# A fused two-layer trunk with a 16-expert mixture: experts put in order of their token count on the chip, the small ones run as plain fp32 products in two column halves

## The chip, the cores and the metric

The kernel runs on one core of a Trainium2 chip. The metric is the device time of one execution in microseconds (us). Its engines are named in the profile as PE (matrix products), PEld (the loads of PE's stationary operand), DVE (elementwise work), ACT (activations and copies), POOL (here mostly indirect DMA) and SP (which issues nearly all of the other DMAs, in order).

## What the kernel computes

Two layers of a trunk: each has a mixer of three branches over 256 tokens of x and 256 of a context, and then a mixture of experts. Layer 0's mixture runs over 512 tokens (x and context), layer 1's over 256 (x alone). The change concerns the mixture:

```python
def hierarchical_moe(h, w_router_group, w_router_expert, w1, w3, w2):
    g_logits = (h @ w_router_group).astype(jnp.float32)
    g_sel = jnp.argmax(g_logits, axis=-1)                      # one of 4 groups
    ...
    top_vals, top_idx = lax.top_k(e_in_group, MOE_TOPK)        # 2 of its 4 experts
    top_w = jax.nn.softmax(top_vals, axis=-1) * g_gate
    ...
    for e in range(MOE_EXPERTS):                               # 16
        hid = jax.nn.silu(h @ w1[e]) * (h @ w3[e])             # 1024 -> 512
        out = out + (hid @ w2[e]) * gates[:, e:e + 1]          # 512 -> 1024
    return out
```

Everything is fp32, to fp32 accuracy. With these inputs the router gives the 16 experts of layer 0 101, 88, 84, 83, 82, 80, 76, 67, 65, 61, 56, 53, 39, 32, 29 and 28 tokens (in falling order), and those of layer 1 75, 69, 42, 39, 36, 31, 28 (four times), 22, 20, 19, 18, 17 and 12.

## The kernel before

Only the routed tokens of an expert are computed, in up to `CAP` = (128, 96) slots per expert in layers 0 and 1. Experts run in the order 0 to 15. For each one POOL gathers its token rows from DRAM (`gather`, L1466), PE transposes them (`tokens`, L1523), and the result is split into a high and a low part. All weights are fp32 and come in pieces of 1 MB (`wload`, L221): two for w1, two for w3, two for w2, so six per expert and 96 per layer. SP issues them in a fixed order (`pieces_of`, L1239), w1's first piece half an expert ahead. A piece is issued when a slot of the ring of buffers is free; some 13 slots in layer 0 and 14 in layer 1 are filled ahead of the routing, and four of them leave the ring after 50 pieces (`CUT`).

Each half piece is split on the chip into a high and a low part (`split`): ACT rounds it (L241, `whi`), DVE subtracts (L242, `wlo`). Every 128x512 tile of a weight then takes three products:

```python
    def mm3(self, out, lh, ll, rh, rl, start, stop):
        mm(out, lh, rh, start=start, stop=False)               # L211
        mm(out, lh, rl, start=False, stop=False)               # L212
        self.mm = mm(out, ll, rh, start=False, stop=stop)      # L213
```

That is 72 products for an expert: 24 for w1, 24 for w3 (`up`, L1528) and 24 for w2. Between them stand 8 transposes of the tokens, tanh on ACT (L1547), two multiplications on DVE (L1548, L1549) and 4 transposes of the hidden rows (L1552). The output rows, scaled by the gate (`ye`, L1586), are scattered to DRAM (`yb`, L1471). The last two experts' rows stay on chip (L1593, L1594); the other rows are read back (L1601), added in pairs on POOL (L1602), and PE puts both together (L1613, L1616), which is the head of a tail of some 15 us in the last layer.

Routing, before all this: one-hot choices on DVE, a prefix count by products on PE (L1394, L1397), the first expert's tokens selected by products with a one-hot (L1415), the slot lists of four experts (one-hots on DVE L1442, products on PE L1444), then token numbers `tki` (L1452) for the gathers. If any expert has more than `CAP` tokens, a branch (L1621) computes the rest in a general way; with these counts it is not taken.

The order on each engine comes from a scheduler that works from its own estimates; PE, DVE and SP run their queues strictly in it.

## Time and profile before

| what | value |
|---|---|
| time, median of 3 runs | 1622.67 us (1621.13 to 1624.53) |
| span of the profiled execution | 1619.3 us |
| PE busy in it | 94% |
| DVE busy | 74% |
| ACT busy | 60% |
| granted TensorE clock, mean | 0.982 of full |

The span runs from the first to the last instruction; the 3.4 us to the median lie around it. The profile has no total time of the profiled execution of its own beside the span, so sums below are made in the span and carried over to the median with those 3.4 us. A busy share is a mean over all stages: what a stage costs is read from its own stretch. The two mixtures run from about 640 to 948 us and from about 1303 to 1602 us.

### The profile page before, as it was taken

What the parts mean: (1) busy time and instruction counts of PE and PEld (TensorE: products, weight loads), DVE (VectorE), ACT (ScalarE), POOL (GpSimd) and SP (SyncE); (2) the same over time, 40 slices, a digit from 0 to 9 for tenths busy, and PEclk for the clock granted to TensorE, in tenths of its full rate; (3) what the DMA queues carried; (4) which work ended last, traced back from release to release, by engine and by line L of the source; (5) the groups of instructions that cost most, each with busy time, mean ns of one, the idle gap of its engine ahead of it and who ended that gap; (6) DMA issues with size and microseconds to landing.
All of it is one profiled execution on the core that took longest, in us unless ns stands there. A gap on an engine that the chain in (4) does not pass through costs nothing. (4 is left out here: it accounts for less than half of the span.)

```text
span 1619.3 us, 23310 instructions
## 1 busy us (share of the span) xinstructions
PE 1518.8 (94%) x8530; PEld 1163.3 (72%) x8530; DVE 1197.5 (74%) x1943; ACT 971.8 (60%) x1530; POOL 245.5 (15%) x244
## 2 busy tenths in 40 slices
PE   6999899999999996999999979998999799999996
PEld 4666665677777796778888748777799767767763
DVE  4479677432476766999999966478855689999996
ACT  4668465322223333888888835577744468888883
POOL 2034100000121103111111031032011121101011
PEclk9999999999999998999999989999999899999999
DMA  9762333443456586999799836223244979989991
GB/s 314 227 195 79 131 105 105 147 150 121 153 180 213 176 301 247 334 374 373 283 371 372 312 112 189 79 79 105 82 145 155 364 269 367 365 303 322 368 362 40
DMA packets 219215, 363.05 MB, mean 224 GB/s; under 512 B 26405, under 2 KB 101359, under 8 KB 219092
## 3 DMA queue, kind: packets, MB, share of 16 engines
q1 hardware_dynamic: 211232, 349.68, 62.7%
q0 software_dynamic: 7424, 11.67, 2.1%
q8 instruction: 71, 1.16, 0.3%
q14 instruction: 52, 0.43, 0.1%
q10 hardware_dynamic: 436, 0.10, 0.0%
HBM read 352.97 MB, written 23.40 MB: 232 GB/s over the span
## 5 line engine op out<-in xcount | busy, mean ns | idle before, releaser
L242 DVE TENSOR_TENSOR wlo<-wraw,whi 128x1024 fp32r<-128x1024 f32 (+1 forms) x514 | 615.3, 1216 | 153.7 <-ACT whi L241 89.1
L241 ACT ACTIVATE whi<-wraw 128x1024 fp32r<-128x1024 f32 (+1 forms) x514 | 523.4, 1029 | 271.0 <-PE pa L205 116.1
L204 PE MATMUL pa<-hhi,whi 128*128 128x512 f32 (+1 forms) x704 | 241.1, 357 | 1.6 <-ACT kT L768 0.8
L205 PE MATMUL pa<-hlo,whi 128*128 128x512 f32 (+1 forms) x704 | 238.4, 353 | 0.1
L212 PE MATMUL pa<-wlo,xh 128*128 128x512 f32 (+1 forms) x480 | 194.6, 405 | 3.0 <-DVE wlo L242 2.8
L211 PE MATMUL pa<-whi,xh 128*128 128x512 f32 (+1 forms) x480 | 191.0, 398 | 0.2 <-ACT xh L247 0.2
L213 PE MATMUL pa<-whi,xl 128*128 128x512 f32 (+1 forms) x480 | 189.6, 395 | 0.0
L204 PEld LDWEIGHTS pa<-hhi,whi 128*128 128x128 f32 x704 | 133.8, 190 | 36.2 <-issue 16.1
L207 PE MATMUL pa<-hhi,wlo 128*128 128x512 f32 (+1 forms) x704 | 151.2, 348 | 0.0
L205 PEld LDWEIGHTS pa<-hlo,whi 128*128 128x128 f32 x704 | 134.0, 190 | 23.1 <-issue 9.6
L207 PEld LDWEIGHTS pa<-hhi,wlo 128*128 128x128 f32 x704 | 113.4, 189 | 20.2 <-issue 6.2
L212 PEld LDWEIGHTS pa<-wlo,xh 128*128 128x128 f32 (+1 forms) x480 | 84.0, 175 | 31.8 <-DVE wlo L242 8.3
L212 PE MATMUL c<-wlo,hh 128*128 128x512 f32 (+1 forms) x256 | 101.5, 396 | 3.7 <-DVE wlo L242 3.7
L211 PEld LDWEIGHTS pa<-whi,xh 128*128 128x128 f32 (+1 forms) x480 | 83.9, 175 | 26.3 <-ACT xh L247 0.3
L739 POOL TENSOR_TENSOR m<-m,gu 128x512 f32<-128x512 f32 (+1 forms) x32 | 39.8, 1242 | 406.0 <-DVE gu L737 406.0
L213 PEld LDWEIGHTS pa<-whi,xl 128*128 128x128 f32 (+1 forms) x480 | 84.2, 175 | 21.6
L211 PE MATMUL c<-whi,hh 128*128 128x512 f32 (+1 forms) x256 | 97.7, 398 | 0.4 <-ACT hh L247 0.2
L1466 POOL DMA_INDIRECT xg<-h2b,tki x30 | 45.8, 1528 | 343.4 <-PE c L1523 285.9
L212 PE MATMUL pa<-y,whi 128*128 128x512 f32 (+1 forms) x192 | 66.8, 348 | 0.9 <-DVE y L248 0.9
L211 PE MATMUL pa<-y,whi 128*128 128x512 f32 (+1 forms) x192 | 66.1, 345 | 0.7 <-DVE mx L1119 0.7
L213 PE MATMUL pa<-y,wlo 128*128 128x512 f32 (+1 forms) x192 | 65.5, 342 | 0.0
L325 DVE SCALAR_TENSOR_TENSOR adaw<-adaw,cT 128x512 f32<-128x512 f32 x56 | 47.1, 842 | 17.4 <-DMA adaw<-in_w_ada_dram 16.8
(471 smaller groups left out, 2807.2 us busy)
## 6 DMA issues: line engine op xcount, KB each, us to landing
wraw<-in_w_dram SPq DMA_DIRECT2D x182, 1024.0 KB
wraw<-in_w_in_dram SPq DMA_DIRECT2D x44, 1024.0 KB
adaw<-in_w_ada_dram SPq DMA_DIRECT2D x80, 512.0 KB
x<-in_w_dram SPq DMA_DIRECT2D x10, 1024.0 KB
adaw<-in_w_ada_dram SPq DMA_DIRECT2D x8, 1024.0 KB
wraw<-in_w_out_dram SPq DMA_DIRECT2D x8, 1024.0 KB
yb<-zero SPq DMA_DIRECT2D x12, 512.0 KB
wraw<-yb SPq DMA_DIRECT2D x6, 1024.0 KB
```

The source lines that it names most:

```text
L204: mm(out, lh, rh, start=(i == 0), stop=False)
L205: mm(out, lh, rl, start=False, stop=False)
L207: self.mm = mm(out, ll, rh, start=False, stop=(i == len(ops) - 1))
L211: mm(out, lh, rh, start=start, stop=False)
L212: mm(out, lh, rl, start=False, stop=False)
L213: self.mm = mm(out, ll, rh, start=False, stop=stop)
L241: self.sp = nc.scalar.activation(hv[:, :, q], v[:, :, q], AF.Copy)
L242: self.sl = self.lo.tensor_sub(lv[:, :, q], v[:, :, q], hv[:, :, q].bitcast(F32))
L325: nc.vector.scalar_tensor_tensor(v[:, j], v[:, j], ck, acc, op0=OP.mult, op1=OP.add)
L739: nc.gpsimd.tensor_add(self.m[:, j, :], self.m[:, j, :], u[:, :TY])
L1466: return nc.gpsimd.indirect_dma_start(out=xgs[e % len(xgs)][:cap], out_offset=None, in_=h2b, in_offset=bass.IndirectOffsetOnAxis(ap=tki[:c ...
```

## The change

All experts keep their six 1 MB pieces. The 16 experts of a layer get *places*, given by a string: `B` for a place whose expert runs as before (128 slots, split weights, 72 products) and `s` for a small place. In layer 0 five of the places are small, in layer 1 eleven. The first two places of layer 0 (three of layer 1) always hold experts 0, 1 (and 2), so that their weights can be loaded ahead of the routing; the others are given out by token count, ranked on the chip, the largest to the `B` places. SP then reads the expert's number from memory into a register (L1272) and addresses the weight pieces with it. The fallback branch is taken if a place holds more than its slots (128 or 64); with these counts it is not.

An expert at a small place has 64 slots and no split: its weights go into the products as they are, as plain fp32. Its 64 tokens fill half of the array's columns; w1 is multiplied in columns 0 to 63 and w3 in columns 64 to 127, and the two column halves of w2's 1024 outputs likewise (`pair`, L1643). That makes 24 products in 12 pairs in place of 72, 8 transposes of 64 rows, a copy of w3's half (ACT), and 4 transposes of the hidden rows; the output rows are scattered as half rows. In the routing the prefix count for expert 0 alone comes first, then the ranking on DVE, and then a second prefix count over the places. The diff, cut to its core:

```diff
-CAP = (128, 96)
+CAP = (128, 128)
+SM = 64
+
+STAT = (2, 3)
+PLACES = ("BBsBBsBBsBBsBsBB", "BBBsssssssssssBB")
...
+    pos = np.zeros((P, 2, 5, NE), f)
+    for l in range(2):
+        big = np.array([x == "B" for x in PLACES[l]])
+        pos[:, l, 0] = NE - 1 - np.arange(NE) + 1.0e5 * np.maximum(0, STAT[l] - np.arange(NE))
+        pos[:, l, 1] = place_ranks(l)
+        pos[:, l, 2] = np.where(big, CAP[l], SM)
+        pos[:, l, 3] = np.where(big, 1, 2)
+        pos[:, l, 4] = (~big)[None, :] * (np.arange(P) >= SM)[:, None]
...
+    n = STAT[l] + PLACES[l][STAT[l]:].count("B")
+    big, small = iter(range(n)), iter(range(n, NE))
+    return [next(big if x == "B" else small) for x in PLACES[l]]
...
+        def src(w, q):
+            if q < STAT[l]:
+                return self.io[w][l, q]
+            if q not in self.eid:
+                self.eid[q] = self.nc.values_load(self.idi[0:1, q:q + 1], engines=(mybir.EngineType.SP,),
+                                                  min_val=0, max_val=NE - 1)
+            return self.io[w][l][bass.ds(self.eid[q], 1)].rearrange("e r c -> (e r) c")
...
+        def begin(q):
+            for w in ("w1", "w3")[:1 + (PLACES[l][q] == "s")]:
+                yield up(w, q, 0)
+        self.eid = {}
+        yield from begin(0)
+        for q in range(NE):
+            yield up("w1", q, 1)
+            if PLACES[l][q] == "B":
+                yield up("w3", q, 0)
+            yield up("w3", q, 1)
+            if q + 1 == STAT[l]:
+                yield from down(q)
+            if q + 1 < NE:
+                yield from begin(q + 1)
+            if q + 1 != STAT[l]:
+                yield from down(q)
...
-        pc = self.c2()
+        self.behind(self.rest, V.tensor_add(Mb, O[:, 0], O[:, 1]))
+
+        def prefix(pc, m, n):
+
+            for t in range(nt):
+                for u in range(t + 1):
+                    nc.tensor.matmul(pc[:, ts(t, n)], self.trilb if u == t else self.onesb, m[:, u, :n],
+                                     start=(u == 0), stop=(u == t))
+        p0 = self.c2()
+        prefix(p0, Mb, 1)
...
+            nc.tensor.matmul(p0[:, ts(1, NE)], self.onesb, Mb[:, u, :], start=(u == 0), stop=(u == nt - 1))
+
+        pm0 = tl([P, nt], "pm0")
+        V.scalar_tensor_tensor(pm0, p0[:, :nt], 1.0, Mb[:, :, 0], op0=OP.add, op1=OP.mult)
...
+        V.scalar_tensor_tensor(key, p0[:, ts(1, NE)], float(NE), pos[:, 0], op0=OP.mult, op1=OP.add)
+        cmp = self.xp.tile(kb, F32, name="cmp")
+        V.tensor_tensor(cmp, key[:, None, :].to_broadcast(kb), key[:, :, None].to_broadcast(kb), op=OP.is_gt)
+        V.reduce_sum(rank, cmp, axis=AX.X)
+        V.tensor_tensor(cmp, rank[:, None, :].to_broadcast(kb), pos[:, 1][:, :, None].to_broadcast(kb), op=OP.is_equal)
+        V.tensor_tensor(cmp, cmp, self.iotab[:, None, :NE].to_broadcast(kb), op=OP.mult)
+        idf = tl([P, NE], "idf")
+        V.reduce_sum(idf, cmp, axis=AX.X)
+        self.idi = tl([P, NE], "idi", I32)
+        V.tensor_scalar(self.idi, idf, -1.0, None, op0=OP.add)
...
+        V.tensor_tensor(Q, O, rank[:, None, None, :].to_broadcast(rb), op=OP.mult)
+        V.reduce_sum(rk, Q, axis=AX.X)
+        V.tensor_tensor(Q, rk[:, :, :, None].to_broadcast(rb), pos[:, 1][:, None, None, :].to_broadcast(rb), op=OP.is_equal)
+        V.tensor_add(Mb, Q[:, 0], Q[:, 1])
+        pc = self.c2()
+        prefix(pc, Mb, NE)
...
+        V.scalar_tensor_tensor(pm, pcv, 1.0, Mb, op0=OP.add, op1=OP.mult)
...
         def scatter(ye, e):
-            return nc.gpsimd.indirect_dma_start(out=yb, out_offset=bass.IndirectOffsetOnAxis(ap=yki[:cap, e:e + 1], axis=0),
-                                         in_=ye[:cap], in_offset=None, bounds_check=2 * T - 1, oob_is_err=False)
+            out, m = (yb, 1) if big[e] else (yb.rearrange("r (h c) -> (r h) c", h=2), 2)
+            return nc.gpsimd.indirect_dma_start(out=out, out_offset=bass.IndirectOffsetOnAxis(ap=yki[:, e:e + 1], axis=0),
+                                         in_=ye, in_offset=None, bounds_check=2 * m * T - 1, oob_is_err=False)
 
...
+
             xg = xgs[e % len(xgs)]
+            if not big[e]:
+                pt = self.c1()
+                for k in range(KD):
+                    nc.tensor.transpose(pt[:, ts(k, SM)], xg[:SM, ts(k, P)], self.ident[:SM, :SM])
+                xs = mp.tile([P, KD, SM], F32, name="xh", bufs=2)
+                nc.scalar.activation(xs.rearrange("p a b -> p (a b)"), pt, AF.Copy)
...
+        def pair(ps, xs, ws, k0, n):
+
+            for k in range(n):
+                for i, w in enumerate(ws):
+                    nc.tensor.matmul(ps[ts(i, SM)], xs[:, k0[0] + k, :], w[:, k, :], start=(k0[0] + k == 0),
+                                     stop=(k0[0] + k == k0[1] - 1))
...
+        def begin(e, xx):
+            ps = self.pA()
+            if big[e]:
+                up(ps, xx, "w1", e, 0)
+            else:
+                pair(ps, xx, [self.piece_at(w, e, 0) for w in ("w1", "w3")], (0, KD), 4)
+            return ps
...
+            else:
+                th = mp.tile([P, FE], F32, name="th", bufs=2)[:SM]
+                t3 = mp.tile([P, FE], F32, name="th", bufs=2)[:SM]
+                nc.scalar.activation(t3, p1[SM:], AF.Copy)
+                gated(th, p1[:SM], t3)
+                pt = hidden(th, SM)
+                hs = mp.tile([P, 4, SM], F32, name="hh", bufs=2)
+                V.tensor_copy(hs.rearrange("p a b -> p (a b)"), pt)
...
+            if not big[e]:
+                p2 = self.c2()
+                for c in range(2):
+                    w = self.piece_at("w2", e, c)
+                    for k in range(2):
+                        pair(p2, hs, [w[:, k:k + 1, ts(o, 512)] for o in range(2)], (2 * c + k, 4), 1)
+                ye = yp.tile([P, 512], F32, name="ye")
+                nc.scalar.activation(ye, p2, AF.Copy, scale=gsl[:, e:e + 1])
+                put = (ye, e)
+                continue
...
-        with tc.If(n > CAP[l]):
+        with tc.If(n > 0):
```

What stands where on the engines changes in three places. First SP in layer 0, around the end of the pieces that are loaded ahead. Before:

```order
L221 DMA wraw<-in_w_dram 128x4x512
L1314 DMA h2b_4833<-h_4840 128x1024 x3
L221 DMA wraw<-in_w_dram 128x2x1024 x2
L221 DMA wraw<-in_w_dram 128x4x512 x4
```

After (`idi` holds the expert numbers; `h2b` are the normed token rows that the gathers read):

```order
L245 DMA wraw<-in_w_dram 128x2x1024
L1366 DMA h2b_4838<-h_4845 128x1024 x3
L245 DMA wraw<-in_w_dram 128x2x1024
L1272 TENSOR_LOAD idi
L1272 ISA x2
L245 ISA
L245 DMA wraw<-in_w_dram 128x4x512
L245 ISA
L245 DMA wraw<-in_w_dram 128x4x512
```

Twelve pieces stand ahead of the first read of a number; each later expert has one such read, and each of its pieces one more instruction ahead of it. The second place is PE near the first products of layer 0, where the rows of expert 1 (the first gather) are transposed; `whi` and `wlo` in the place of the tokens are expert 0's. Before, after 23 of expert 0's products:

```order
L211 MATMUL pa<-whi 128x512
L212 MATMUL pa<-wlo,whi 128x512
L1523 MATMUL c_5766<-ident,xg_5610 128x128 x4
L1523 MATMUL c_5773<-ident,xg_5610 128x128 x4
L213 MATMUL pa<-whi,wlo 128x512
```

After the change, after 17 of them, and those of expert 2 seven products later:

```order
L236 MATMUL pa<-wlo,whi 128x512
L1627 MATMUL c_5815<-ident,xg_5648 128x128 x4
L1627 MATMUL c_5822<-ident,xg_5648 128x128 x4
L237 MATMUL pa<-whi,wlo 128x512
L235 MATMUL pa<-whi 128x512
L236 MATMUL pa<-wlo,whi 128x512
L237 MATMUL pa<-whi,wlo 128x512
L235 MATMUL pa<-whi 128x512
L236 MATMUL pa<-wlo,whi 128x512
L237 MATMUL pa<-whi,wlo 128x512
L1618 MATMUL c_6032<-ident,xg_5650 128x64
```

The transposes moved six products forward. The third place is PE in layer 1, at an expert in the middle. Before, the change from one expert's w2 to the next one's tokens (`hh` are the hidden rows):

```order
L211 MATMUL c_13618<-whi,hh 96x512
L212 MATMUL c_13618<-wlo,hh 96x512
L213 MATMUL c_13618<-whi,hl__13585 96x512
L211 MATMUL pa<-whi,xh 96x512
L212 MATMUL pa<-wlo,xh 96x512
L213 MATMUL pa<-whi,xl 96x512
```

After, a whole small expert takes a few rows (`pa` w1 and w3, `c` in the row from `hh` w2):

```order
L1662 MATMUL c_13523<-ident,th 128x64 x4
L1643 MATMUL pa<-wraw,xh 64x512 x3
L1643 MATMUL c_13559<-wraw,hh 64x512 x8
L1643 MATMUL pa<-wraw,xh 64x512 x8
L1618 MATMUL c_13586<-ident,xg_12731 128x64 x8
L1618 MATMUL c_13665<-ident,xg_12733 128x64 x8
```

The three products for each weight tile, with both parts of the weights, are gone, and the raw pieces `wraw` go into the array.

## Rows read from the trace of the kernel before

**Rows 1.** The page's busy times (us, share, instructions), PE and DVE.

```profile
PE 1518.8 (94%) x8530; PEld 1163.3 (72%) x8530; DVE 1197.5 (74%) x1943; ACT 971.8 (60%) x1530; POOL 245.5 (15%) x244
```

**Rows 2.** Stretches: busy us (instructions) by engine, granted clock, DMA share, GB/s.

```profile
core 0: us, PE busy (x) PEld busy (x) DVE busy (x) ACT busy (x) POOL busy (x), PEclk, DMA share, GB/s
...
600.00:619.00 19.00, 18.52 (x162) 18.42 (x160) 9.51 (x19) 8.39 (x21) 1.11 (x2) 1.00 1.04 391
620.00:640.00 20.00, 8.32 (x65) 8.17 (x66) 17.67 (x68) 4.90 (x9) 10.59 (x8) 0.66 0.69 250
...
660.00:780.00 120.00, 119.99 (x594) 96.43 (x594) 116.88 (x155) 101.55 (x118) 16.44 (x13) 1.00 1.02 372
...
800.00:900.00 100.00, 100.00 (x468) 81.19 (x467) 94.46 (x97) 85.53 (x102) 12.35 (x10) 1.00 1.01 366
...
1262.00:1290.00 28.00, 23.51 (x189) 22.67 (x188) 17.46 (x28) 14.17 (x34) 2.59 (x2) 0.92 1.04 395
1330.00:1420.00 90.00, 90.00 (x446) 63.57 (x445) 85.22 (x100) 76.59 (x92) 14.95 (x11) 1.00 1.02 365
1470.00:1560.00 90.00, 90.00 (x425) 63.22 (x424) 84.01 (x87) 76.93 (x90) 9.66 (x8) 1.00 1.02 364
```

**Rows 3.** Waits of SP from 600 to 960 us: total us, times, longest.

```profile
SPq L221 <- DVE wlo L242: 220.1, 76, 15.3
```

**Rows 4.** Timeline of ACT: tanh of experts 1 and 11 (layer 0), 1 and 14 (layer 1).

```profile
672.09 0.58 ACT L1547 ACTIVATE th<-pa 128x512 f32<-128x512 f32 x1
855.32 0.59 ACT L1547 ACTIVATE th<-pa 128x512 f32<-128x512 f32 x1
1333.25 0.59 ACT L1547 ACTIVATE th<-pa 96x512 f32<-96x512 f32 x1
1566.01 0.59 ACT L1547 ACTIVATE th<-pa 96x512 f32<-96x512 f32 x1
```

**Rows 5.** Timeline of PE: products with split weights (start, modelled length).

```profile
1436.01 0.40 PE L212 MATMUL c<-wlo,hh 128*96 128x512 f32 x1
1436.24 0.39 PE L213 MATMUL c<-whi,hl__14312 128*96 128x512 f32 x1
```

**Rows 6.** Chain that ended last: two plain fp32 products of 512 columns.

```profile
1604.66 0.86 PE pa L1616 x2
```

**Rows 7.** Timeline of PE: plain fp32 products in two column halves, and in four column quarters.

```profile
222.96 1.94 PE L1137 MATMUL c<-PT,vc 128*64 128x256 f32 x14
57.05 1.92 PE L803 MATMUL pa<-hhi,wdraw 128*32 128x512 f32 x16
```

**Rows 8.** By source line, ns min/median/max: SP's issue of a piece; SP's read of a number.

```profile
L221 SPq DMA_DIRECT2D wraw<-in_w_dram x182: 367/368/5155, 587.4 to 1562.5; - x182
L1621 SPq TENSOR_LOAD <-cnti x2: 303/395/487, 919.6 to 1570.3; - x2
```

**Rows 9.** Timeline at the start of layer 0's experts (PE, POOL, then SP).

```profile
633.27 9.29 PE L1415 MATMUL c<-oh,h 128*128 128x128 f32 x64 [0.73 <-DVE oh L1409]
633.63 2.69 DVE L1442 TENSOR_SCALAR pe<-iotab,pm 128x128 bf16<-128x128 bf16 x16
644.90 1.27 POOL L1466 DMA_INDIRECT xg<-h2b,tki  x1 [13.40 <-DVE yki L1454]
652.85 1.04 PE L1523 MATMUL c<-ident,xg 128*128 128x128 f32 x8
```

**Rows 10.** Timeline of SP: pieces that it issued, with the stretch from first to last.

```profile
633.00 42.75 SPq L221 DMA_DIRECT2D wraw<-in_w_dram  x11
...
647.89 0.37 SPq L221 DMA_DIRECT2D wraw<-in_w_dram  x1
...
1308.59 0.37 SPq L221 DMA_DIRECT2D wraw<-in_w_dram  x1
```

**Rows 11.** The page's DMA queues: packets, MB; q0 carries the gathers and scatters.

```profile
q0 software_dynamic: 7424, 11.67, 2.1%
```

**Rows 12.** Timeline at the layers' ends: last outputs on ACT, sums on POOL.

```profile
945.50 1.39 ACT L1593 ACTIVATE wraw<-c,gsl 128x512 fp32r<-128x512 f32 x2 [2.44 <-PE c L213]
930.31 5.78 POOL L1602 TENSOR_TENSOR wraw<-wraw 128x1024 f32<-128x1024 f32 x2 [22.91 <-DMA wraw<-yb]
1601.01 1.38 ACT L1593 ACTIVATE wraw<-c,gsl 96x512 fp32r<-96x512 f32 x2 [2.43 <-PE c L213]
```

More of the change, by code (lines that the diff above doesn't have):

```diff
@@ L170, in setup_late @@
         nc.vector.tensor_scalar(self.iotab, io_, 1.0, None, op0=OP.add)
+        for i in range(2):
+            nc.vector.tensor_copy(self.iotas[:, ts(i, SM)], self.iotab[:, :SM])
         tr = tp.tile([P, P], F32, name="tr")
@@ L1257, in splits_of @@
-    def splits_of(self):
-        n = 5
-        for v, a in self.pieces:
-            for u in range(2):
-                yield self.split(v[:, ts(u, a), :], a, 1024 // a, 4 if n > 3 else 1)
-            n = max(1, n - 1)
+        def src(w, q):
[5 more added lines that the diff above has]
+            return self.io[w][l][bass.ds(self.eid[q], 1)].rearrange("e r c -> (e r) c")
@@ new lines, in piece_at, with halves @@
+    def piece_at(self, *key):
+        while key not in self.got:
+            k, v = next(self.pieces)
+            self.got[k] = v
+        return self.got.pop(key)
+    def halves(self, *key):
+        if key in self.cut:
+            yield from self.cut.pop(key)
+            return
+        v, a = self.piece_at(*key), 1 if key[0] == "w2" else 2
+        self.parts = max(1, self.parts - 1)
+        for u in range(2):
+            yield self.split(v[:, ts(u, a), :], a, 1024 // a, 4 if self.parts > 3 else 1)
@@ L1345, in moe_ahead @@
         self.pieces = chain(first, gen)
-        gen = self.splits_of()
-        self.wsp = chain([next(gen) for _ in range(2)], gen)
+        self.got, self.cut, self.parts = {}, {}, 6
+        self.cut["w1", 0, 0] = list(self.halves("w1", 0, 0))
     def moe(self, l):
@@ L1353, in moe @@
         ns, cap = T // SEQ, CAP[l]
+        big = [x == "B" for x in PLACES[l]]
         dp, h2b, yb, lg = self.dp, self.h2b, self.yb, self.lg
@@ L1417, in moe @@
             self.evict_hl(*(x[:, ts(c, 4)].rearrange("p a b -> p (a b)") for x in xx), pt[:, :4 * cap])
+        pos = self.pos
+        kb, rb = [P, NE, NE], [P, 2, nt, NE]
+        key, rank = tl([P, NE], "key"), tl([P, NE], "rank")
+        V.scalar_tensor_tensor(key, p0[:, ts(1, NE)], float(NE), pos[:, 0], op0=OP.mult, op1=OP.add)
[8 more added lines that the diff above has]
+        V.tensor_scalar(self.idi, idf, -1.0, None, op0=OP.add)
+        Q = tl(rb, "Q")
+        rk = tl([P, 2, nt], "rk")
+        V.tensor_tensor(Q, O, rank[:, None, None, :].to_broadcast(rb), op=OP.mult)
[4 more added lines that the diff above has]
+        prefix(pc, Mb, NE)
+        for u in range(nt):
+            nc.tensor.matmul(pc[:, ts(nt, NE)], self.onesb, Mb[:, u, :], start=(u == 0), stop=(u == nt - 1))
+        pm = tl([P, nt, NE], "pm")
+        pcv = pc[:, :nt * NE].rearrange("p (t e) -> p t e", t=nt)
+        V.scalar_tensor_tensor(pm, pcv, 1.0, Mb, op0=OP.add, op1=OP.mult)
+        vals = tl([P, nt, NE, 3], "vals", BF)
+        V.tensor_copy(vals[:, :, :, 2], Q[:, 1])
+        nc.gpsimd.tensor_copy(vals[:, :, :, 0], self.small[:, 4:5][:, :, None].to_broadcast([P, nt, NE]))
+        for t in range(nt):
+            nc.gpsimd.memset(vals[:, t, :, 1], float(t) - BIGI / P)
         self.sx.close()
@@ L1526, in tokens, with up, gated, hidden @@
             return xh, xl
-        def up(ps, xx, c):
-            for u in range(2):
-                wh, wl = next(self.wsp)
+        def up(ps, xx, w, e, c):
+            for u, (wh, wl) in enumerate(self.halves(w, e, c)):
                 for k in range(2):
                     kk = 4 * c + 2 * u + k
-                    self.mm3(ps[:cap], xx[0][:, kk, :], xx[1][:, kk, :], wh[:, k, :], wl[:, k, :], kk == 0, kk == KD - 1)
+                    self.mm3(ps, xx[0][:, kk, :], xx[1][:, kk, :], wh[:, k, :], wl[:, k, :], kk == 0, kk == KD - 1)
+        def pair(ps, xs, ws, k0, n):
[10 more added lines that the diff above has]
+            return ps
+        def gated(th, p1, p3):
+            nc.scalar.activation(th, p1, AF.Tanh, scale=0.5)
+            V.scalar_tensor_tensor(th, th, 1.0, p1, op0=OP.add, op1=OP.mult)
+            V.tensor_mul(th, th, p3)
+        def hidden(th, n):
+            pt = self.c3()
+            for k in range(4):
+                nc.tensor.transpose(pt[:, ts(k, n)], th[:, ts(k, P)], self.ident[:n, :n])
+            return pt[:, :4 * n]
         yes = []
-        p1 = self.pA()
-        up(p1, xx, 0)
+        p1 = begin(0, xx)
         for e in range(NE):
-            up(p1, xx, 1)
+            if big[e]:
+                up(p1, xx, "w1", e, 1)
+            else:
+                pair(p1, xx, [self.piece_at(w, e, 1) for w in ("w1", "w3")], (4, KD), 4)
             if e == 0:
@@ L1576, in moe @@
                 rq = self.pool(sr, "rows2", bufs=2, side="right") if nt > 2 else None
-            p2 = [self.c2(), self.c2()]
-            for k in range(4):
-                wh, wl = next(self.wsp)
-                for o in range(2):
-                    self.mm3(p2[o][:cap], hh[:, k, :], hl[:, k, :], wh[:, 0, ts(o, 512)], wl[:, 0, ts(o, 512)],
-                             k == 0, k == 3)
+            if not big[e]:
+                p2 = self.c2()
+                for c in range(2):
+                    w = self.piece_at("w2", e, c)
[5 more added lines that the diff above has]
+                continue
+            p2 = [self.c2(), self.c2()]
+            for c in range(2):
+                for u, (wh, wl) in enumerate(self.halves("w2", e, c)):
+                    k = 2 * c + u
+                    for o in range(2):
+                        self.mm3(p2[o], hh[:, k, :], hl[:, k, :], wh[:, 0, ts(o, 512)], wl[:, 0, ts(o, 512)],
+                                 k == 0, k == 3)
             if e < NE - 2:
```

106 lines of the change are left out of this document (48 added, 58 removed).

## Prediction

> **What bounds the kernel now.** The busy times come first [rows 1]: PE 94%, DVE 74%. As means over all stages they don't say which stage has slack, so I cut the span into stretches [rows 2]. Look there at three columns, PE, DMA share and GB/s. In both mixtures (660 to 780 and 800 to 900 us; 1330 to 1420 and 1470 to 1560 us) PE is busy all the time, DVE for 116.88 of 120 us in the first, and the DMA engines are at a share of 1.01 to 1.02 with 364 to 372 GB/s. Where weights are loaded without a slot having to come free (600 to 619 and 1262 to 1290 us) the share is 1.04 and the rate 391 and 395 GB/s. So PE paces the experts and the weight stream runs only 5 to 8% below its own best. The waits of SP say the same from the other side [rows 3]: 76 times, 220 us in all, it waits for DVE's last split of a piece, that is for a ring slot, not for a transfer.
>
> The period of an expert is read from its tanh [rows 4]: layer 0 (855.32 - 672.09) / 10 = 18.3 us, layer 1 (1566.01 - 1333.25) / 13 = 17.9 us. It is made of products that start 0.23 us apart [rows 5]: 72 x 0.23 = 16.6 us, the rest being transposes.
>
> **What a small expert costs on PE.** Plain fp32 products of 512 columns: two take 0.86 us [rows 6], 0.43 each, twice a split product's 0.23. Column parts run side by side [rows 7]: 14 products of 256 columns in halves take 1.94 us; less about 0.4 for the end of the last, that is 0.22 a pair, the price of one alone (half of 0.43). Sixteen of 512 columns in quarters take 1.92 us: about 0.43 for four. So 12 pairs x 0.43 = 5.2 us. Add 12 transposes at half the rows, under 1 us, and a switch of the column tiling: 6.5 us. The chain between w3 and w2 (a copy, tanh at 0.59 [rows 4], two multiplications, an eviction) is covered in layer 0 by the neighbours' products; where small experts follow each other only the next one's first half (1.7 us) covers it, so I take 8 us in layer 1. The bounds are 6 and, if the halves ran one after the other, 12 us.
>
> PE then needs 11 x 18.3 + 5 x 6.5 = 234 us in layer 0, in place of 16 x 18.3 = 293, and 5 x 18.3 + 11 x 8 = 180 in layer 1, in place of 286. Splits fall with it, 12 of each on ACT and DVE per small expert, so DVE does not become the bound.
>
> **What the weights cost.** They stay: 96 x 1.0486 MB = 100.7 MB a layer, and they decide now. At 385 GB/s a piece takes 2.72 us and the six of an expert, big or small, 16.3, and with its share of gathers and scatters (11.67 MB in all [rows 11], some 7.6 in layer 0 by its number of tokens) 17 to 17.7. I take 385, close under the free-running 391 and 395, since the gathers' and scatters' small rows go beside it; the ends are 366 (no faster than now) and 395.
>
> The Trainium skill, "DMA: Bandwidth & Descriptors", section Specifications, gives about 358 GB/s as a core's share of HBM; the rows at 364 to 395 lie above it in every loaded stretch, so the measurement decides here. By that figure the sum below would come to some 30 us more.
>
> **What the routing costs.** Ranking and second prefix are about 15 small DVE operations and 20 tiny products. They run while PE selects expert 0's tokens (633.27 to 642.56 [rows 9]), so that selection covers them; without it they would cost about 5 us. Not covered is what follows: the second prefix stands behind that selection on PE, so the 16 one-hots (2.69 us [rows 9], done long before now) come after 643, and the first gather goes out some 3.6 us later than 644.90. In the row of PE its transposes moved up from 23 to 17 products in; today they stand at 652.85 [rows 9], just when the rows have landed, some 8 us after the gather's issue. Then PE gets there near 650 and waits until about 656; gathers 2 and 3 follow in the same way. Queued behind are expert 0's products, and for these the ring slots and so SP. I take a delay of 6 us in layer 0 (bounds 3 and 10). In layer 1 the transposes stand behind all 48 first products, so only the 4 us of the later gather.
>
> SP: a read of a number takes 0.30 to 0.49 us, a piece's issue 0.37 [rows 8], and each piece gets one more instruction. Unknown in the trace is what that one and a register in the address cost; between nothing and a second issue (0.37) the whole is about 1 us a piece against 2.72 of transfer, so it hides. The first read stands where today the 14th piece waits for a slot until 647.89 [rows 10]; the ranks are ready by then.
>
> **The sum, layer 0.** Today 22 pieces are issued by 675.75 (11 ahead, 11 in the row [rows 10]). With the delay: 681.5. The other 74 and the one under way are 78.6 MB, with 7 MB of gathers and scatters 85.6 MB: 222 us at 385 GB/s, so the last piece lands near 904. PE alone would be through by 649 + 234 = 883, so the stream decides by about 20 us. After the last piece two splits, 12 products and the outputs remain, 8 us: 912. But the readback of the other experts' rows stands behind the last weights on SP: four more MB, and then POOL's sums, 5.78 us for two [rows 12]. Today these end 9 us ahead of the last outputs (930.31 + 5.78 against 945.50 [rows 12]); now they come to about 914. So 945.5 - 914.5 = 31 us gained. That four slots leave the ring after 50 pieces costs nothing if the stream is by then behind; the cover is that the ring, full at the start, loses about 9 us of stock per three places (3 x 17.2 against 18.3 + 18.3 + 6.5), and it would cost up to two pieces (5 us) if it did.
>
> **The sum, layer 1,** on today's clock. Three big experts pace it first: tanh of the second at 1333.25 [rows 4], the third 18 later, its end 8 behind that, 4 for routing: 1362. By then 18 pieces are used and the ring of 14 is nearly refilled (the 15th went out at 1308.59 [rows 10]): 31 issued. 65 remain, 68.2 MB and 3 MB of rows: 185 us at 385, so 1547. The last outputs follow at 1555, readback (2 MB, 5.4 us) and sums at 1559. Today the last outputs end at 1602.4 [rows 12] and the first product with the read rows is at 1604.66 [rows 6], so the gain is 45 us. The last 15 us stay.
>
> 31 + 45 = 76. The sum is made in a span of 1619.3; with the 3.4 us around it, the median is 1622.7 - 76 = 1546.7. With the estimates of delay rounded upward in both layers I take **1545 us**.
>
> **The rivals.**
> 1. *The stream is no faster under load than now.* For it: over long stretches the share is already 1.01 to 1.02 [rows 2]. Against: 391 and 395 with the same kind of pieces. At 366 GB/s the 157 MB of both sums cost 429 us in place of 408: 1566. Chance 0.18.
> 2. *The halves don't overlap, or fp32 costs more.* Small experts then take 12 to 13 us: layer 0 is through on PE at about 649 + 266 = 915, just level with the stream, layer 1 unchanged: about 1550. Beside it stands a rule: the Trainium skill, "FP8 and Floating Point Precision", TensorE Precision Notes, speaks of four passes for true fp32; 0.43 against 0.23 [rows 5, 6] is about two of the split products, so no row here shows four. With 0.86 a pair the small expert is at 12 us as well. Chance 0.05.
> 3. *The clock falls.* From 620 to 640 us PE is busy 8.32 of 20 us and the granted clock is 0.66 [rows 2], a mix of the two levels, 2.4 and 1.2 GHz. In layer 1 the small experts leave PE busy some 8 of 17 us, so there it could fall too. At 1.2 GHz they take up to 16 us, still inside 17, but the last two big ones start slowly: up to 10 us more, 1555. Chance 0.09.
> 4. *Slower than before:* a piece addressed from a register is issued, or its transfer prepared, so slowly that SP becomes the pace. Today a piece comes every (945.5 - 647.89) / 83 = 3.6 us; more than 3.6 in place of 0.37 [rows 8] turns the sign. At 4 us the 140 pieces cost 140 x 0.4 = 56 us more than before: 1679. Nothing in the trace shows such a load; this kernel's rows have only fixed addresses. Chance 0.04.
> 5. *No effect:* the DMA engines are the bound already (share 1.02) and PE's work is only stretched over it. Against it speak SP's waits for slots [rows 3]. Time 1620 to 1624. Chance 0.03.
>
> **How the numbers follow.** The forecast holds 0.61. With 395 GB/s both sums fall by 10 us, with half the routing delay by 5 more and a count of pieces that is off by three by 8: 1520. At the top stands the stream at 366 with the clock's 10 us: 1576. So 1520 to 1577. A measurement of this kernel can tell about 0.2%, 3.2 us, from no change: faster 0.93, same 0.03, slower 0.04.
>
> **What would show it.** In the profile after: a DMA share near 1.04 with 380 to 395 GB/s from about 700 to 900 us and through the small experts of layer 1; PE busy in well under 60% there, waiting for pieces; SP no longer waiting for DVE's splits; pairs of L1643 starting together, 0.43 us apart; PE idle around 650 to 656. I am wrong if the rate stays at 366, if SP's row shows gaps between a read and the next piece, or if the layers end well behind the last weights.

## The result, and the profile after

The changed kernel takes 1602.27 us (median of 4 runs, 1596.48 to 1606.12) against 1621.9 us for the kernel before beside it: a ratio of 0.9874 with a 95% interval of 0.9847 to 0.9902. It is 20 us faster, and the forecast was 76. The direction was right, the size was not, and 1602 lies far outside 1520 to 1577.

The busy times of the page, which answer to [rows 1]:

```profile
PE 1465.3 (91%) x8165; PEld 1038.6 (65%) x8165; DVE 972.2 (61%) x1771; ACT 765.4 (48%) x1306; POOL 237.7 (15%) x244
```

DVE lost 225 us and ACT 206, as the removed splits say, but PE only 53. The ends of the two layers (ACT's last outputs, the rows that answer to [rows 12]) show where:

```profile
958.66 1.39 ACT L1739 ACTIVATE wraw<-c,gsl 128x512 fp32r<-128x512 f32 x2 [2.44 <-PE c L237]
...
1582.76 1.38 ACT L1739 ACTIVATE wraw<-c,gsl 128x512 fp32r<-128x512 f32 x2 [2.37 <-PE c L237]
```

Layer 0 ends 13 us *later* than before (958.66 against 945.50), where 31 us earlier were forecast. The profiled execution is the longest of the four (1606.12 us); in a run with the same layer 0 (`e2_layer1_all_big` below) the last outputs stand at 952.74, so the loss is 7 to 13 us. From there to the end of layer 1 it is 624.1 us in place of 655.5: 31 us gained, 45 forecast. Stretches of the same execution, with the columns of [rows 2]:

```profile
660.00:700.00 40.00, 38.77 (x195) 25.56 (x194) 32.13 (x60) 26.14 (x31) 5.53 (x5) 0.99 0.83 292
700.00:780.00 80.00, 80.00 (x402) 54.23 (x401) 62.32 (x90) 53.95 (x64) 10.80 (x9) 1.00 1.04 394
780.00:860.00 80.00, 75.84 (x354) 47.10 (x352) 49.47 (x55) 45.79 (x57) 11.23 (x10) 0.99 0.94 344
860.00:920.00 60.00, 52.66 (x182) 29.68 (x181) 27.81 (x37) 23.42 (x30) 2.94 (x3) 0.84 0.91 331
...
1400.00:1560.00 160.00, 136.40 (x639) 56.51 (x635) 38.72 (x61) 39.27 (x57) 17.24 (x17) 0.96 1.04 396
```

In layer 1 the stream does what was forecast, 1.04 and 396 GB/s through the small experts, though PE is busy for 85% of that stretch (136.40 of 160 us) and not for well under 60%. In layer 0 the stream does so only from 700 to 780 us; then the rate falls back to 344 and 331, PE is less busy, and the granted clock is 0.84 at the end. From 600 to 960 us SP still waits 118.7 us for splits on DVE (220.1 in [rows 3]), where the prediction saw no such waits. PE is 100% busy from 700 to 780 although five of sixteen experts were to cost it a third. Tanh in that stretch, with a small expert in the middle (64 rows):

```profile
728.75 0.59 ACT L1655 ACTIVATE th<-pa 128x512 f32<-128x512 f32 x1
749.95 0.59 ACT L1655 ACTIVATE th<-pa 64x512 f32<-64x512 f32 x1
762.09 0.60 ACT L1655 ACTIVATE th<-pa 128x512 f32<-128x512 f32 x1
780.19 0.59 ACT L1655 ACTIVATE th<-pa 128x512 f32<-128x512 f32 x1
```

Three places take 51.4 us. Less twice 18.3 for the big ones (the period before the change), the small one costs 14.8, not 6.5. Its products are seen best in the timeline of PE:

```profile
694.34 3.65 PE L1643 MATMUL pa<-wraw,xh 128*64 128x512 f32 x16
697.92 0.50 PE L235 MATMUL pa<-whi,xh 128*128 128x512 f32 x1
...
1490.69 0.64 PE L1643 MATMUL pa<-wraw,xh 128*64 128x512 f32 x1 [1.63 <-DMA wraw<-in_w_dram]
1490.70 0.64 PE L1643 MATMUL pa<-x,xh 128*64 128x512 f32 x1
1491.17 0.59 PE L1643 MATMUL pa<-wraw,xh 128*64 128x512 f32 x1
1491.18 0.59 PE L1643 MATMUL pa<-x,xh 128*64 128x512 f32 x1
1491.60 0.59 PE L1643 MATMUL pa<-wraw,xh 128*64 128x512 f32 x1
1491.61 0.59 PE L1643 MATMUL pa<-x,xh 128*64 128x512 f32 x1
```

The first row is one half of w1 and w3, which is eight products in the program's order, yet it counts x16: the profile has two records for each plain fp32 product. So it is over the whole kernel: the 16 small experts have 16 x 24 = 384 products, and L1643 has 768 records (464, 256 and 48 by tile). Four pairs take 3.58 us (694.34 to 697.92), 0.86 to 0.9 a pair. In layer 1, where the two halves lie in tiles of different names, the records of a pair start 0.01 us apart and the next step follows 0.43 later: the halves do run side by side. With two records for a product, each product takes two steps of 0.43.

PE's waits in layer 0, with the kind of wait, us in total, times and the longest:

```profile
PE pa L235 <- ACT whi L265: 8.7, 6, 2.3
PE pa L236 <- DVE wlo L266: 4.1, 5, 1.9
PE c L236 <- DVE wlo L266: 2.6, 3, 1.1
```

They are waits for the splits of a big expert. ACT's timeline, and PE's, at the change from the last small expert to a big one show why:

```profile
897.66 0.59 ACT L1655 ACTIVATE th<-pa 64x512 f32<-64x512 f32 x1
898.15 1.99 ACT L265 ACTIVATE whi<-wraw 128x1024 fp32r<-128x1024 f32 x2
900.05 1.06 ACT L271 ACTIVATE xh<-c 128x512 fp32r<-128x512 f32 x2
911.12 0.69 ACT L1719 ACTIVATE ye<-c,gsl 128x512 f32<-128x512 f32 x1 [10.02 <-PE c L1643]
911.71 2.94 ACT L265 ACTIVATE whi<-wraw 128x1024 fp32r<-128x1024 f32 x3
...
899.25 0.50 PE L235 MATMUL pa<-whi,xh 128*128 128x512 f32 x1 [2.27 <-ACT whi L265]
...
912.80 0.49 PE L235 MATMUL pa<-whi,xh 128*128 128x512 f32 x1 [1.72 <-ACT whi L265]
...
915.08 0.63 PE L235 MATMUL pa<-whi,xh 128*128 128x512 f32 x1
915.51 0.63 PE L236 MATMUL pa<-wlo,xh 128*128 128x512 f32 x1
...
921.18 0.39 PE L236 MATMUL pa<-wlo,xh 128*128 128x512 f32 x1
921.41 0.40 PE L237 MATMUL pa<-whi,xl 128*128 128x512 f32 x1
```

The big expert's first splits (898.15) are queued behind the small expert's tanh, and PE waits 2.27 us for them. Then ACT stands for 10 us at the small expert's output `ye`, which needs all of its w2 products; PE is busy for most of that time, but the big expert's next splits (911.71) are queued behind `ye`, and PE waits another 1.72 us. At 915 us it works at the lower of its two clock levels, 1.2 GHz (products 0.43 us apart), before it is back at 2.4 GHz at 921 (0.23).

### The profile page after: what moved, and what is told of

It is laid out like the page before. It is cut to its first block, busy times and chain, and to the rows that moved or that the text cites. A ratio compares the mean times of both kernels' runs of the same rounds, so it can differ in the third digit from the quotient of the medians.

```text
span 1604.3 us, 22319 instructions
## 1 busy us (share of the span) xinstructions
PE 1465.3 (91%) x8165; PEld 1038.6 (65%) x8165; DVE 972.2 (61%) x1771; ACT 765.4 (48%) x1306; POOL 237.7 (15%) x244
## 5 line engine op out<-in xcount | busy, mean ns | idle before, releaser
L266 DVE TENSOR_TENSOR wlo<-wraw,whi 128x1024 fp32r<-128x1024 f32 (+1 forms) x334 | 402.5, 1218 | 205.9 <-ACT whi L265 130.3
L265 ACT ACTIVATE whi<-wraw 128x1024 fp32r<-128x1024 f32 (+1 forms) x334 | 332.2, 1011 | 264.0 <-PE pa L229 120.8
L1643 PE MATMUL pa<-wraw,xh 128*64 128x512 f32 x464 | 132.7, 613 | 2.9 <-DMA wraw<-in_w_dram 2.5
L235 PE MATMUL pa<-whi,xh 128*128 128x512 f32 x224 | 94.6, 422 | 13.4 <-ACT whi L265 12.7
L236 PE MATMUL pa<-wlo,xh 128*128 128x512 f32 x224 | 96.5, 431 | 9.0 <-DVE wlo L266 8.9
L1656 DVE SCALAR_TENSOR_TENSOR th<-th,pa 128x512 f32<-128x512 f32 (+1 forms) x32 | 21.8, 680 | 130.7 <-ACT th L1655 130.7
L237 PE MATMUL pa<-whi,xl 128*128 128x512 f32 x224 | 93.1, 416 | 0.0
L1643 PEld LDWEIGHTS pa<-wraw,xh 128*64 128x64 f32 x464 | 37.6, 139 | 67.5 <-issue 59.5
L1643 PE MATMUL c<-wraw,hh 128*64 128x512 f32 x256 | 70.3, 601 | 0.0
L235 PEld LDWEIGHTS pa<-whi,xh 128*128 128x128 f32 x224 | 44.8, 200 | 33.1 <-ACT whi L265 18.8
```

The source lines that it names most:

```text
L265: self.sp = nc.scalar.activation(hv[:, :, q], v[:, :, q], AF.Copy)
L266: self.sl = self.lo.tensor_sub(lv[:, :, q], v[:, :, q], hv[:, :, q].bitcast(F32))
L1643: nc.tensor.matmul(ps[ts(i, SM)], xs[:, k0[0] + k, :], w[:, k, :], start=(k0[0] + k == 0), stop=(k0[0] + k == k0[1] - 1))
L1656: V.scalar_tensor_tensor(th, th, 1.0, p1, op0=OP.add, op1=OP.mult)
```

## The experiments

The theory after the result: a plain fp32 product costs 0.86 us and not 0.43; what a small expert still saves at that price is lost in layer 0 to waits behind ACT's order; and at a layer's end the last two experts lag behind the stream. The rivals were the overhead (ranking, second prefix, register addresses), the stream, and the halves of the array. Each ratio is to the kernel before, on the same chip. The change itself was not timed again beside these runs, so a difference to it ("16 us less") is one of medians from different sessions, in which the kernel before moved by 1.8 us (1621.22 to 1622.98); by the ratios such a difference comes out 1 to 3 us smaller.

### Which layer, and which part of the change

`e1_layer0_all_big`, `e2_layer1_all_big` and `e3_all_big` change only the string of places:

```diff
-PLACES = ("BBsBBsBBsBBsBsBB", "BBBsssssssssssBB")
+PLACES = ("BBBBBBBBBBBBBBBB", "BBBsssssssssssBB")
...
+PLACES = ("BBsBBsBBsBBsBsBB", "BBBBBBBBBBBBBBBB")
...
+PLACES = ("BBBBBBBBBBBBBBBB", "BBBBBBBBBBBBBBBB")
```

> All places of layer 0 are big (no small expert there); layer 1 stays as in the change. Theory A (a plain fp32 product of 512 columns keeps PE 0.86 us, not 0.43, and what a small expert still saves is lost again to splits that come late behind it and to a lower clock): the five small ones cost on average 20 us each against 18.3 of a big one, so layer 0 ends 5 to 10 us earlier than with the change, about 1595 us (ratio 0.983). Rival B (small experts do save in layer 0, and routing or register addresses ate it): 5 x 6 us are lost, about 1630 us (ratio 1.005).

Measured: 1602.55 us, ratio 0.988 (0.9859 to 0.9901), the same as with the change. The five small experts of layer 0 neither save nor lose: nearer to theory A than to B, but the 5 to 10 us that it wanted are not there.

> All places of layer 1 are big; layer 0 stays as in the change. Theory A: the 27 us that layer 1 gains come from its eleven small experts, so they are lost, and what is left is layer 0's loss of 13: about 1630 to 1635 us (ratio 1.006). Rival B: the layers' gains come from the order by count or from the mixer between them, and about 1605 us remain.

Measured: 1630.87 us, 1.0059 (1.0041 to 1.0077). All of the gain is layer 1's, as theory A has it. Layer 0 is the same program as in the change, and it ends 6 us earlier in this execution than in the change's, at a higher clock (0.98 in place of 0.95, see below), level with the all-big layer 0 of `e1_layer0_all_big` (952.36):

```profile
952.74 1.39 ACT L1739 ACTIVATE wraw<-c,gsl 128x512 fp32r<-128x512 f32 x2 [2.46 <-PE c L237]
```

> Ranking, second prefix and register-addressed loads stay, no expert is small in either layer: the price of the overhead by itself. Theory A: 6 us in layer 0 and 4 in layer 1 from the later gathers, register addresses nothing: about 1631 us (ratio 1.006). Rival B: a register-addressed piece costs more than its transfer hides; with 1 us more on each of 160 pieces 1700 us or more.

Measured: 1633.84 us, 1.0078 (1.0059 to 1.0097), 11 us more than the kernel before beside it (1622.98). Ranking, later gathers, register addresses and the 128 slots in place of 96 in layer 1 together cost about what the prediction had, 10 us. Where they cost it is another matter: by the traces 8 us lie in layer 0 (its last outputs at 953.49 against 945.50) and 1 us in layer 1 (656.7 us from there to its last outputs, against 655.5), where 6 and 4 were forecast. SP's reads of a number are short, and the issue of a piece hardly grew (0.38 us in place of 0.37); by source line, of the changed kernel:

```profile
L1272 SPq TENSOR_LOAD <-idi x27: 263/273/511, 633.4 to 1527.2; - x27
L245 SPq DMA_DIRECT2D wraw<-in_w_dram x182: 136/380/6631, 584.7 to 1544.8; - x182
```

With e3 as the base, the small experts of layer 1 are worth 31 us (e3 against e1), those of layer 0 from 0 (e1 against the change) to 3 us (e3 against e2).

### The price of a product

`e4_half_products`:

```diff
             for k in range(n):
+                if (k0[0] + k) % 2:
+                    continue
                 for i, w in enumerate(ws):
                     nc.tensor.matmul(ps[ts(i, SM)], xs[:, k0[0] + k, :], w[:, k, :], start=(k0[0] + k == 0),
-                                     stop=(k0[0] + k == k0[1] - 1))
+                                     stop=(k0[0] + k == k0[1] - 2))
```

> The small experts leave out every second of their products (the odd row tiles of w1, w3 and w2), so that PE needs about 5.2 us for them, which is the price that the prediction had; loads, transposes, splits, copies and order stay. Theory A: layer 0 gains some 5 x 5 us on PE plus a part of the stalls, layer 1 a few us until the weight stream bounds it: 1560 to 1575 us (ratio 0.967). Rival B (the loss is in ACT's order, the clock or the stream, not in the products): 1590 us or more.

Measured: 1578.62 us, 0.9738 (0.9718 to 0.9759): 24 us less than the change, a little above theory A's span. At the price that the prediction had set, 24 of the missing 57 us come back, 15 to 21 of them in layer 0 (its last outputs at 937.87). The other 33 are not in the products.

`e10_one_column_half` takes work out of one half of the columns alone:

```diff
+            m = k0[1] // 2
             for k in range(n):
                 for i, w in enumerate(ws):
+                    kk = k0[0] + k
+                    if i and kk % m:
+                        continue
```

> Of the products in columns 64 to 127 only every fourth (w1, w3) or second (w2) is left; those in columns 0 to 63 all stay, loads and all else too. Theory A (the two halves run side by side, and a pair costs 0.86 us because one plain fp32 product does): no change, 1598 to 1606 us. Rival B (a product costs 0.43 us, as the prediction had it, and the halves run one after the other): the small experts get 8 x 0.43 = 3.4 us shorter, layer 0 some 17 us, about 1583 us.

Measured: 1595.77 us, 0.985 (0.9831 to 0.9869). The time alone lies between the two spans and decides nothing: its interval meets that of the change, and that the pieces of w3 now free their slots after fewer products, which might give some us, was not tested. The timeline decides. Where the row of the change counts 16 records in 3.65 us, here three products of the first half stand beside one of the second, and one stands alone between other work:

```profile
688.23 1.07 PE L1647 MATMUL pa<-wraw,xh 128*64 128x512 f32 x2
...
696.25 2.79 PE L1647 MATMUL pa<-wraw,xh 128*64 128x512 f32 x8
698.97 0.50 PE L235 MATMUL pa<-whi,xh 128*128 128x512 f32 x1
```

The four take 2.72 us to the next start, 0.9 for each of the three steps, with or without a partner. At 0.43 one after the other, four would have taken 1.7. The one alone has two records and takes 1.00 us to the next start (689.23); that the 0.14 over 0.86 are the switches of the column tiling around it is an estimate. So a partner in the other columns is free, and a lone product costs some 0.9 us, not 0.43.

### ACT's order

`e5_splits_first` changes the order on ACT. The first two splits of a big expert that follows a small one are made ahead of the small one's copy of w3's half and its tanh (`behind` orders an instruction after `self.sp`, which is the last split on ACT in both kernels), and the small one's output is put off until after the splits of the big one's first w3 piece. Between two small experts the output is put off too, behind the next one's copy:

```diff
+                if big[e + 1]:
+                    self.cut["w1", e + 1, 0] = list(self.halves("w1", e + 1, 0))
...
-                nc.scalar.activation(t3, p1[SM:], AF.Copy)
+                cp = nc.scalar.activation(t3, p1[SM:], AF.Copy)
+                if big[e + 1]:
+                    self.behind(cp, self.sp)
+                put_late()
...
+                i = nc.scalar.activation(ye, late[0], AF.Copy, scale=gsl[:, late[1]:late[1] + 1])
+                if b:
+                    self.behind(i, self.sp)
```

> Only the order on ACT is changed against the change: the first two splits of a big expert that follows a small one stand ahead of the small one's tanh, and the small one's scaled output stands behind the first half of the big one's w3. Theory A (part of layer 0's loss is PE waiting for splits that stand in ACT's row behind a small expert's tanh and output, 15 us of waits between 660 and 960): 8 to 12 us less, about 1592 us (ratio 0.981). Rival B (PE has only its products to blame, the waits would move elsewhere): 1599 to 1603 us.

Measured: 1585.82 us, 0.9792 (0.9771 to 0.9814): 16 us less (13 by the ratios), more than theory A had. By the traces 12 to 17 us of it lie in layer 0, whose last outputs now stand at 941.14. PE's waits for splits in layer 0 fell to

```profile
PE pa L236 <- DVE wlo L266: 3.9, 5, 1.7
PE pa L235 <- ACT whi L265: 2.9, 3, 2.2
PE c L236 <- DVE wlo L266: 1.5, 2, 0.9
```

8.3 us in all from 15.4. The granted clock of 660 to 960 us is higher too, 0.95 with the change (first) and 0.99 here (second). But in `e2_layer1_all_big` (third), with the change's layer 0 and waits of 14.9 us, it is 0.98. So the waits went with the order; how much of the clock did is open.

```profile
660.00:960.00 300.00, 282.58 (x1262) 182.36 (x1260) 203.03 (x266) 171.84 (x204) 36.75 (x28) 0.95 0.89 328
```

```profile
660.00:960.00 300.00, 283.21 (x1308) 183.88 (x1307) 214.44 (x281) 177.70 (x214) 44.28 (x33) 0.99 0.89 331
```

```profile
660.00:960.00 300.00, 281.24 (x1273) 179.31 (x1273) 205.57 (x274) 171.73 (x204) 36.21 (x28) 0.98 0.90 331
```

`e6_small_in_a_row` leaves ACT's order and puts the string of layer 0 to `"BBBBBBBBBsssssBB"`.

> The five small places of layer 0 stand in a row ahead of the last two big ones, so that a big expert follows a small one once and not five times. Theory A (each change from small to big costs about 3 us of waits for splits, and more at the low clock): about 10 us less, 1592 us. Rival B (the weight stream decides: five small ones in a row run at its pace of 17 us, and what they save on PE is lost there): 1600 us or more.

Measured: 1590.25 us, 0.9811 (0.9793 to 0.983), 12 us less. Fewer changes from small to big do nearly the same, by another way.

`e11_first_and_row` is e5 with e6's string.

> The order on ACT of the run with the splits first, and the five small places of layer 0 in a row. Theory A (both cure the same waits behind a change from small to big): no more than the splits first alone, 1583 to 1590 us. Rival B (the row cures something else too, such as the switches of the clock): 1575 us.

Measured: 1584.31 us, 0.977 (0.9747 to 0.9794): hardly more than e5 alone, so both cure the same loss.

### The end of a layer

`e7_light_last_two` yields no low part for the last two experts, and `mm3` then makes one product:

```diff
+            if key[1] >= NE - 2:
+                h = self.hl.tile([P, 1024], F32R, name="whi")
+                hv = h.rearrange("p (a b) -> p a b", a=a)
+                self.sp = self.nc.scalar.activation(hv, v[:, ts(u, a), :], AF.Copy)
+                yield hv, None
+                continue
```

> The last two experts of both layers leave out their low parts: one product in place of three for a weight tile and no subtraction on DVE; loads, order and all else stay. Theory A (after the last weights have landed PE and the splits are still a whole expert behind, since the two last big ones take 18 us each whatever the stream does): layer 0 ends about 12 us earlier, layer 1 about 15: about 1576 us (ratio 0.971). Rival B (the end of a layer follows the last weights and the readback): within 5 us of the change, 1597 to 1602 us.

Measured: 1571.37 us, 0.9689 (0.9668 to 0.9711): 31 us less than the change, more than theory A's 26. SP's timeline in the changed kernel, beside the outputs at 958.66 and 1582.76:

```profile
915.17 8.70 SPq L245 DMA_DIRECT2D wraw<-in_w_dram  x3
924.00 2.11 SPq L1747 DMA_DIRECT2D wraw<-yb  x4
...
1547.34 0.97 SPq L245 DMA_DIRECT2D x<-in_w_dram  x1
1548.42 2.46 SPq L1747 DMA_DIRECT2D wraw<-yb  x2
```

From the issue of the last piece to the outputs it is 35 us in both layers, and not the 8 us after its landing that the prediction gave. In `e7_light_last_two`, layer 1:

```profile
1530.56 0.98 SPq L248 DMA_DIRECT2D x<-in_w_dram  x1
...
1551.40 1.27 ACT L1748 ACTIVATE wraw<-c,gsl 128x512 fp32r<-128x512 f32 x2 [0.59 <-PE c L236]
```

The last piece goes out as long after the first tanh as in the change (223 us after 1307.19, against 224), but the outputs follow it by 21 us, not 35. So layer 1's 14 us lie wholly behind the last weights: its end hangs on the last two experts' work on PE and DVE. In layer 0 the outputs follow by 24 us, not 35 (918.07 to 941.75). The kernel before has the same lag in layer 1, 35 us to its outputs at 1601.01 [rows 12]. PE sets the pace there, but the row was there to ask how 35 should become 8:

```profile
1565.72 0.37 SPq L221 DMA_DIRECT2D x<-in_w_dram  x1
```

### All three, and a better kernel

`e9_three_together` joins the edits of e4, e5 and e7.

> Half the products of the small experts left out, the splits first on ACT, and the last two experts without their low parts, all in one. Theory A (the price of a product, ACT's order and the lag of the last two experts are the whole difference between 1602 and the forecast of 1545): close to the forecast, 1533 to 1548 us; less than the sum of the three steps (24 + 16 + 31 would give 1531), since the weight stream bounds it. Rival B (something else is lost as well, such as a slower start of the stream): 1555 us or more.

Measured: 1549.87 us, 0.9555 (0.9541 to 0.9569), 5 us from the forecast and 2 above theory A's span. The stretches, with the kernel before (second fence) beside it:

```profile
680.00:920.00 240.00, 216.71 (x951) 140.37 (x949) 157.13 (x213) 157.51 (x190) 28.20 (x24) 0.94 1.02 385
1330.00:1500.00 170.00, 122.32 (x474) 44.18 (x472) 31.62 (x71) 35.44 (x56) 19.95 (x20) 0.82 1.04 391
```

```profile
680.00:920.00 240.00, 238.40 (x1157) 192.09 (x1156) 229.10 (x273) 202.17 (x234) 29.26 (x23) 1.00 0.95 346
```

With PE out of the way, layer 0's stream runs at 385 GB/s, the very value that was assumed. The three steps add up to 71 us by themselves and 52 together: with all of them the stream sets the pace in both layers (385 and 391 GB/s), so what a step frees beyond that would not be seen. This kernel leaves out work, so it bounds what the three are worth and is no kernel to use.

`e8_fixed_layer0` takes the ranking, the second prefix and the register addresses out of layer 0:

```diff
-STAT = (2, 3)
-PLACES = ("BBsBBsBBsBBsBsBB", "BBBsssssssssssBB")
+STAT = (16, 3)
+PLACES = ("BBBBBBBBBBBBBBBB", "BBBsssssssssssBB")
...
+        if stat:
+            prefix(p0, Mb, NE)
```

> Layer 0 as before the change (experts 0 to 15 in order, all big, no ranking, no second prefix, fixed addresses), layer 1 as in the change, and ACT's order of the run with the splits first. Theory A (layer 0's ranking and addresses cost 8 us and its small experts save nothing): 8 to 12 us less than with the change, 1590 to 1594 us, faster than both kernels. Rival B (small experts in layer 0 save what the overhead costs): 1600 us or more.

Measured: 1588.15 us, 0.9801 (0.9787 to 0.9816), 14 us less than the change. In its trace layer 0's last outputs stand at 946.80, 6 to 12 us before those of the change's layer 0, and layer 1 takes 623.5 us against 624.1. So most of it is layer 0, where the overhead is gone; the mended order in layer 1, which e8 has as well, does not show in this execution.

`e12_seven_small` is e5 with `"BBsBsBsBsBsBssBB"` in layer 0.

> The splits first, and seven small places in place of five in layer 0 (all experts with at most 64 tokens). Theory A (with the order mended a small expert saves PE some 4 to 5 us, and the stream is not yet the bound in layer 0): 5 to 9 us less than with five, 1577 to 1581 us. Rival B (the stream or the lag behind it decides already): 1584 to 1588 us.

Measured: 1584.39 us, 0.9776 (0.9763 to 0.9789), the same as with five small ones: theory A missed. From 680 to 920 us the stream runs at 370 GB/s in e5 and at 376 here, near the 385 of e9. Which of the two, the stream or the lag of the last experts, takes the rest of layer 0 was not taken apart further.

Of the kernels that compute all of it, e5, e11 and e12 are the fastest, 1584 to 1586 us, 2.1 to 2.3% below the kernel before and 1% below the change.

## Why the prediction was wrong

**The price of a small expert: the step that failed first.** "Two take 0.86 us [rows 6], 0.43 each" read two records as two products. They are the two steps of one. The same slip is in the reading of [rows 7]: 14 records are seven products, so a pair of 256 columns takes two steps of 0.22. The overlap of column parts was right, the price of what overlaps was half the true one: 12 pairs x 0.86 = 10.3 us, and 14.8 us with transposes and switches, against 6.5. A look at the program's order next to the trace would have shown it: the row counts twice what the order counts. Rival 2 had this price, but treated it as a matter of 5 us, because the step "PE alone would be through by 883" then moved only to 915 and met the stream. With 14.8 us it moves to 649 + 11 x 18.3 + 5 x 14.8 = 924, 20 us behind the stream. The price is worth 24 us (e4). The rule that stood beside it, four passes for true fp32 in the Trainium skill, "FP8 and Floating Point Precision", TensorE Precision Notes, agrees with what the trace shows: 0.86 is 3.7 times the 0.23 of a split product [rows 5].

**The chain between the stages was priced, ACT's order was not.** "Covered in layer 0 by the neighbours' products" held for the chain itself, but ACT is a queue: a big expert's splits stand behind a small expert's tanh and output, and these wait for PE. That is a wait which the change itself adds, and the prediction named nobody who queues behind it. It is worth 13 to 16 us (e5). Rival 3 had looked for a lower clock in layer 1 alone; it fell in layer 0 as well (0.84 from 860 to 920 us), by how much through this order is open.

**"After the last piece two splits, 12 products and the outputs remain, 8 us"** assumed that PE stands ready for every piece. Two big experts at the end take 36 us on PE, the stream brings them in 33, and what PE is behind by then is behind at the end too. For layer 1 the end was 17 us later than worked out (its last outputs ended 261 us after its first tanh, 244 had been worked out), though the last weights went out when forecast: 224 us after the first tanh (1323.51 to 1547.34), and 232 to their landing had been worked out. e7 shows that the end follows these two experts' work. Its 31 us contain work that a kernel needs, so they are not a size of the error.

**What held.** The stream's own rate: 385 assumed, 394 and 396 in the loaded stretches, 385 in e9. So rival 1 fell, and also rival 5. The overhead: 10 us forecast, 11 measured (e3), so rival 4 fell; register addresses cost nothing that shows. That the sums agree is partly luck, since the layers' shares (8 and 1) are not those forecast (6 and 4). In layer 0 the second tanh came 6.3 us later (678.40 against 672.09 [rows 4]), 6 forecast, but not by the way described, so this too is luck: the first gather went out at 645.75, only 0.85 later than in [rows 9], and PE's two waits for gathered rows are short.

```profile
645.75 1.43 POOL L1555 DMA_INDIRECT xg<-h2b,tki  x1 [16.81 <-DVE yk L1540]
...
651.81 1.06 PE L1627 MATMUL c<-ident,xg 128*128 128x128 f32 x8 [1.45 <-DMA xg<-h2b,tki]
...
655.74 0.24 PE L1618 MATMUL c<-ident,xg 64*128 64x64 f32 x1 [1.26 <-DMA xg<-h2b,tki]
```

These are 2.7 of the 6.3 us; the others were not traced to one cause.

**The layers.** In layer 0 the forecast of 31 us could not come even with the right price: the kernel before already moves 346 GB/s over 680 to 920 us, so a stream at 385 had some 10% to give there, an estimated 24 us in 240, and the overhead alone took 8 back (e3). With half the products left out (e4) the layer still ended only 8 us earlier than before; that the lag of the last two experts and ACT's order took the rest is argued from e5 and e7, not shown by a run for this layer alone. In layer 1, eleven small experts in a row run at the stream's pace, as forecast.

## What to carry to other kernels

Before a duration of a trace row is divided by its count, the count should be held against the program's own: a kind of instruction may leave two records, and every estimate built on it is then off by a factor of two. When one kind of work is put beside another on in-order engines, what matters is who stands behind the instruction that now waits, on each queue that the edit touches: here the tanh and the outputs of five small experts on ACT undid about all that 240 removed products had freed in layer 0 (e1 and e2 end it at 952, e5 at 941). And a stage that becomes bound by its loads ends when its last consumers are done, so the last consumers should be the light ones; e7 speaks for it by leaving work out, and no run here put small experts last.

## What the runs showed of the hardware

At a granted clock of 1.00 (2.4 GHz), a plain fp32 product of 512 columns takes two steps of 0.43 us and leaves two records, a split product takes one step of 0.23 and leaves one. Two products in the two column halves start 0.01 us apart and the second costs nothing (2.72 us for three with one partner, 3.58 for four with four). One core drew 394 to 396 GB/s from memory for 80 and 160 us at a stretch. A read of a number by SP took 0.27 us, and a load with a register in its address was issued in 0.38 us, about as one with a fixed address (0.37 [rows 8]). The granted clock fell from 1.00 to 0.84 over 860 to 920 us while PE still was busy for 52.66 of 60 us; a second execution of the same layer 0 (e2) had 0.91 there with PE busy for 52.72, and the kernel with the mended order (e5) 0.97 with 55.52.
